# One hybrid decoder layer on eight cores: from two passes of 1024 tokens to one pass of 2064 with weights read once

## The chip, the cores and the metric

The kernel runs on the eight NeuronCores of one Trainium2 chip. Every core does the whole layer for one prompt of 2048 tokens and for 16 decode ("sample") tokens; the cores do not talk to each other. The metric is the device time of the slowest core in microseconds (us), so a few microseconds lost on one core in eight are lost for all.

A program on all eight cores has a second, slower state in some of its executions. Ratios are the mean time of one kernel's fast runs over that of the other's fast runs of the same rounds, so they are not quite the ratio of the medians quoted beside them.

Engines are named as in the profile: PE does matmuls, PEld loads their weights, DVE, ACT and POOL do the elementwise work, SP issues DMA.

## The reference

```python
D_MODEL = 1024; BATCH = 8; SEQ = 2048; DEC_BATCH = 128; D_FF = 2816; EPS = 1e-6
POOL_WINDOWS = (2, 4, 8, 16)

def layer(x, pool_prev, w_in, g_mix, w_pool, s_pool, w_s, b_s, g_v,
          w_pool_out, w_gmlp_out, w_out, g_ffn, w_gate, w_up, w_down):
    h = rmsnorm(x, g_mix)
    proj = h @ w_in                              # 3584 columns: a 512, u 512, v 512, gates 2 x 1024
    a, z = proj[..., :o1], jax.nn.gelu(proj[..., o1:o2])
    gate_a, gate_b = jax.nn.sigmoid(proj[..., o2:o3]), jax.nn.sigmoid(proj[..., o3:])
    pa = pool_mixer(seq_a, pos0, w_pool, s_pool)   # causal means over 2, 4, 8, 16 rows, minus the row,
                                                   # then a 128 x 128 matrix per group, times s_pool
    sg, v = spatial_gating(z, w_s, b_s, g_v)       # u * (causal 128 x 128 mix of rmsnorm(v) + b_s)
    x = x + (gate_a * (pa @ w_pool_out) + gate_b * (sg @ w_gmlp_out)) @ w_out
    h2 = rmsnorm(x, g_ffn)
    x = x + (jax.nn.silu(h2 @ w_gate) * (h2 @ w_up)) @ w_down
    return x, new_pool, v
# then y = rmsnorm(x, g_final); the last 15 rows of a and the normalised v rows are outputs too
```

I call the part up to `pa` and `sg` stage A, then come the gate stage, w_out, and the FFN (gate and up, then down).

## The kernel before

It works in two passes of 1024 tokens (the first takes the 16 samples along) and reads every weight twice. Weights come through a ring of four 8 KB slots, in blocks cut out of the original fp32 arrays and cast to bf16 by the DMA; a slot is refilled when the block in it has been used. The order of every engine is the order in which the program text emits the instructions.

```python
TPS = 1024; NSUP = SEQ // TPS; NSLOT = 4
blocks = []
for s in range(NSUP):
    for cb in (2, 0, 1):
        blocks.append([(0, 8, 512, win_v[:, :, cb * 512:(cb + 1) * 512])])
    ...                                                        # cut: gates, w_pool_out, w_out
    for j in range(NF // 2):
        blocks.append([(0, 8, 256, wgate_v[:, :, j * 256:(j + 1) * 256]),
                       (2048, 8, 256, wup_v[:, :, j * 256:(j + 1) * 256])])
    ...                                                        # cut: w_down
for s in range(NSUP):
    tts = [(i, 128, i * 128) for i in range(8)]                # token tiles of 128
    nts = [(0, 512, [0, 1, 2, 3]), (512, 512, [4, 5, 6, 7])]   # token blocks of 512 columns
    if s == 0:
        tts.append((8, NSMP, TPS)); nts.append((TPS, NSMP, [8]))   # the 16 samples
    ...
    for j in range(NF // 2):                                   # FFN, two rows of 128 at a time
        for fl in range(2):
            for ni, (c0, W, tl) in enumerate(nts):
                bG, bU = h_mm(gw, uw, hres, fl, c0, W, tl)     # 8 + 8 matmuls of W columns
                h_evac(f, c0, W, bG, bU)                       # silu on ACT, product on DVE
        ring_release(hj)
```

The norm takes ACT (sum of squares), DVE (mean plus eps), POOL (`pow`, -0.5), DVE (scale), PE (8 transposes) and ACT (copy out).

## Time and profile before

| | |
|---|---|
| time, median of 3 runs | 885.39 us (880.47 to 886.75) |
| profiled execution, slowest core | 882.3 us |
| PE busy | 94% |
| HBM read | 129.8 MB per core |

The first fence is from the page of the slowest core: busy time per engine, then the span in 40 equal slices of 22 us (each digit is the busy share in tenths; PEclk is the granted PE clock in tenths), the bytes, and the chain of work that ended last.

```profile
PE 830.3 (94%) x4584; PEld 392.5 (44%) x4584; DVE 366.0 (41%) x601; ACT 247.1 (28%) x448; POOL 142.6 (16%) x174
PE   1689999999999999999997999999999999999996
PEclk9989999999999999999999999999999999999999
DMA  8995336666884746266367951567678475455304
HBM read 129.76 MB, written 9.01 MB: 157 GB/s over the span
PE 88%; DMA 5%; DVE 3%; issue 1%; SPq 1%; ACT 1%; POOL 1%; DVEq 0%; POOLq 0%; ACTq 0%
```

PE is nearly always busy, the chain is 88% PE, and DMA is half idle outside the first slices. So the span is PE work plus the places where PE is kept from it. The next fence is the timeline of PE: start, duration, what, and in brackets the idle time before it with what ended it. The rows are from the start, from the boundary of the two passes, and the last one.

```profile
36.33 16.98 PE L346 MATMUL ps<-ring,hT 128*128 128x512 bf16 x72
57.59 6.28 PE L346 MATMUL ps<-hT,ring 128*128 128x512 bf16 x24 [3.94 <-DMA ring<-w_in]
...
77.33 1.89 PE L346 MATMUL ps<-hT,ring 128*128 128x512 bf16 x8
79.06 0.39 PE L638 MATMUL ps<-wsT,ovl 128*128 128x128 bf16 x4
...
480.71 0.61 PE L396 MATMUL ps<-ident_b,hb 128*128 128x128 bf16 x8 [1.45 <-DVE ms L360]
484.04 1.01 PE L396 MATMUL ps<-ident_b,hb 128*128 128x128 bf16 x8 [2.73 <-DVE ms L360]
...
865.76 7.93 PE L346 MATMUL ps<-ring,ovl 128*128 128x512 bf16 x36
```

The first projections start at 36 us and stop again, and PE is dense only from 57.6 us. Eight matmuls of 512 columns take 79.06 - 77.33 = 1.73 us, so the pitch (the time from the start of one to the start of the next) is 216 ns; the mean duration of one (379 ns in the groups by form) is latency, as they overlap. PE ends at 873.7 and the span at 882.3, which is a tail of 8.6 us. At the boundary of the passes there are gaps of 1.45 and 2.73 us, and the clock drops after them. The view of stretches shows that (columns: stretch, its length, busy time and count of PE, PEld, DVE, ACT, POOL, then granted clock, DMA share, GB/s):

```profile
480.60:487.00 6.40, 3.56 (x22) 2.07 (x23) 3.51 (x6) 5.46 (x9) 5.13 (x6) 0.65 0.95 311
```

### The profile page before, as it was taken

The page shows a single profiled execution, that of the slowest core. Times are in us where ns is not written, and L with a number is a line of the kernel's source. Part 1 is how long each engine was busy: PE and PEld are TensorE (multiplying, and loading weights), DVE is VectorE, ACT ScalarE, POOL GpSimd, SP SyncE. Part 2 cuts the span into 40 slices and gives each one's busy share as a digit, 9 for nine tenths or more (in the row PEclk, how much of TensorE's full clock was granted, in tenths as well). Part 3 has the DMA queues.
Part 4 walks back from the last instruction along what each step waited for, and adds up shares of the span by engine and source line. Part 5 has one row for each costly group of instructions (what it writes and reads, how often), then busy time and mean ns, then how long its engine had stood idle before and what let it go on. Part 6 is the DMA issues. An engine that isn't in the chain of part 4 may idle for free.

```text
span 882.3 us, 13022 instructions; the slowest of 8 cores (876.1 to 882.3 us)
## 1 busy us (share of the span) xinstructions
PE 830.3 (94%) x4584; PEld 392.5 (44%) x4584; DVE 366.0 (41%) x601; ACT 247.1 (28%) x448; POOL 142.6 (16%) x174
## 2 busy tenths in 40 slices
PE   1689999999999999999997999999999999999996
PEld 1334444445444444444443444444544444444442
DVE  2448544447322211134557594434631212114446
ACT  3643422225311111120126543222441111110012
POOL 2420011021201010000225201201120101000003
PEclk9989999999999999999999999999999999999999
DMA  8995336666884746266367951567678475455304
GB/s 209 201 141 66 72 39 74 79 102 91 95 97 51 94 51 82 40 93 96 48 139 243 155 66 25 73 82 103 80 87 104 54 90 72 60 84 84 60 18 174
DMA packets 102482, 81.05 MB, mean 92 GB/s; under 512 B 5324, under 2 KB 96964, under 8 KB 102403
## 3 DMA queue, kind: packets, MB, share of 16 engines
q0 software_dynamic: 94048, 58.10, 51.6%
q1 hardware_dynamic: 7390, 20.88, 7.4%
q10 hardware_dynamic: 981, 1.24, 0.6%
q8 instruction: 38, 0.62, 0.3%
q14 instruction: 25, 0.20, 0.1%
HBM read 129.76 MB, written 9.01 MB: 157 GB/s over the span
## 4 chain that ended last, share of the span: by engine, by line
PE 88%; DMA 5%; DVE 3%; issue 1%; SPq 1%; ACT 1%; POOL 1%; DVEq 0%; POOLq 0%; ACTq 0%
PE ps L346 86%; DMA ring<-w_in 2%; DMA xbuf<-xs 2%; PE ps L396 1%; SPq L304 1%; DVE hb L384 1%; DVE ps L644 1%; ACT hT L404 0%; POOL rs L364 0%; DVE shr L536 0%; DVE shr L544 0%; DVE ovl L549 0%; DVE ovl L649 0%; PE ps L593 0%; DVEq L917 0%
## 5 line engine op out<-in xcount | busy, mean ns | idle before, releaser
L346 PE MATMUL ps<-hT,ring 128*128 128x512 bf16 (+1 forms) x2720 | 497.0, 338 | 7.4 <-DMA ring<-w_in 3.9
L346 PEld LDWEIGHTS ps<-hT,ring 128*128 128x128 bf16 x2720 | 228.0, 98 | 263.3 <-issue 11.5
L346 PE MATMUL ps<-ring,ovl 128*128 128x512 bf16 (+1 forms) x1020 | 224.3, 379 | 0.0
L739 DVE TENSOR_TENSOR ovl<-ftmp,ps 128x512 bf16<-128x512 f32 (+1 forms) x110 | 62.3, 583 | 248.4 <-PE ps L346 245.1
L346 PEld LDWEIGHTS ps<-ring,ovl 128*128 128x128 bf16 (+1 forms) x1020 | 97.7, 97 | 118.8 <-issue 4.3
L737 ACT ACTIVATE ftmp<-ps 128x512 f32<-128x512 f32 (+1 forms) x110 | 56.6, 514 | 246.2 <-PE ps L346 246.1
L355 ACT ACTIVATE junk<-xbuf 128x1024 bf16<-128x1024 f32 (+1 forms) x47 | 49.6, 1055 | 139.4 <-DVE xbuf L861 60.7
L364 POOL TENSOR_TENSOR rs<-ms,mhalf 128x1 f32<-128x1 f32 (+1 forms) x68 | 55.5, 819 | 176.4 <-DVE ms L360 176.4
L825 DVE TENSOR_TENSOR xbuf<-xbuf,ps 128x512 f32<-128x512 f32 (+1 forms) x68 | 46.7, 687 | 54.7 <-PE ps L346 54.7
L346 PE MATMUL ps<-ovl,ring 128*128 128x512 bf16 (+1 forms) x320 | 63.2, 337 | 0.0
L707 DVE TENSOR_TENSOR shr<-shr,ps 128x512 f32<-128x512 f32 (+1 forms) x40 | 23.4, 584 | 91.9 <-PE ps L346 91.9
L396 PE MATMUL ps<-ident_b,hb 128*128 128x128 bf16 (+1 forms) x272 | 23.8, 239 | 33.7 <-DVE hb L384 29.3
L267 POOL DMA_DIRECT2D ring<-w_gate x22 | 19.5, 884 | 209.7 <-PE ps L346 209.7
L404 ACT ACTIVATE hT<-ps 128x1024 bf16<-128x1024 bf16 (+1 forms) x34 | 32.3, 966 | 51.3 <-PE ps L396 51.2
L693 ACT ACTIVATE shr<-ps 128x512 f32<-128x512 f32 (+1 forms) x40 | 20.6, 514 | 88.5 <-PE ps L346 87.2
L346 PEld LDWEIGHTS ps<-ovl,ring 128*128 128x128 bf16 x320 | 27.2, 97 | 30.2
L267 POOL DMA_DIRECT2D ring<-w_in x22 | 19.5, 896 | 126.8 <-PE ps L346 116.6
L396 PEld LDWEIGHTS ps<-ident_b,hb 128*128 128x128 bf16 (+1 forms) x272 | 19.3, 108 | 42.1 <-issue 38.6
L267 POOL DMA_DIRECT2D ring<-w_down x12 | 10.3, 858 | 146.0 <-PE ps L346 146.0
L346 PE MATMUL ps<-ring,hT 128*128 128x512 bf16 (+1 forms) x136 | 33.3, 409 | 0.0
L861 DVE TENSOR_TENSOR xbuf<-xbuf,ps 128x512 f32<-128x512 f32 (+1 forms) x34 | 23.2, 683 | 21.7 <-PE ps L346 21.7
L700 ACT ACTIVATE shr<-ps 128x512 f32<-128x512 f32 (+1 forms) x40 | 20.6, 514 | 34.0 <-PE ps L346 33.9
(76 smaller groups left out, 378.9 us busy)
## 6 DMA issues: line engine op xcount, KB each, us to landing
ring<-w_gate POOLq DMA_DIRECT2D x22, 512.0 KB, 8.5
ring<-w_up POOLq DMA_DIRECT2D x22, 512.0 KB, 10.8
xbuf<-xp SPq DMA_DIRECT2D x16, 512.0 KB, 8.7
ring<-w_in POOLq DMA_DIRECT2D x16, 512.0 KB, 10.4
ring<-w_down POOLq DMA_DIRECT2D x8, 1024.0 KB, 10.2
ring<-w_in POOLq DMA_DIRECT2D x6, 1024.0 KB, 18.9
yp<-ybuf SPq DMA_DIRECT2D x11, 512.0 KB, 3.2
ring<-w_out POOLq DMA_DIRECT2D x4, 1024.0 KB, 13.4
```

What stands on the lines that cost most here:

```text
L267: (lambda e, dst=dst, src=src: e.dma_start(out=dst, in_=src)),
L346: ins = e.matmul(out=out, lhsT=lhs_fn(i), rhs=rhs_fn(i), start=(i == 0), stop=(i == n - 1))
L355: P.op('act', lambda e: e.activation(out=junk[:R, ji, 0:width], in_=src_ap, func=AF.Square, accum_out=ss[:R, k:k + 1]), reads=list(src_res ...
L364: P.op('pool', lambda e: e.tensor_tensor(out=rs[:R, k:k + 1], in0=ms[:R, k:k + 1], in1=mhalf[:R, 0:1], op=ALU.pow), reads=[('ms', k), 'mha ...
L396: ins = e.transpose(out=PSB[b][:, kc, :R], in_=hb[:R, hi, kc * 128:(kc + 1) * 128], identity=ident_b[:R, :R])
L404: P.op('act', lambda e: e.activation(out=dst, in_=src, func=AF.Copy), writes=[('hT', slot, 0), ('hT', slot, 1), ('ps', b)])
L693: P.op('act', lambda e, bA=bA, gi=gi, W=W: e.activation(out=gab[:, gi, 0, :W], in_=PS[bA][:, :W], func=AF.Sigmoid), reads=[], writes=[('ga ...
L707: P.op('dve', lambda e, bP=bP, gi=gi, W=W: e.tensor_tensor(out=gab[:, gi, 0, :W], in0=gab[:, gi, 0, :W], in1=PS[bP][:, :W], op=ALU.mult), ...
L737: P.op('act', lambda e: e.activation(out=ftmp[:, fi, :W], in_=PS[bG][:, :W], func=AF.Silu), reads=[], writes=[('ftmp', fi), ('ps', bG)])
L739: P.op('dve', lambda e: e.tensor_tensor(out=actT[:, f, c0:c0 + W], in0=ftmp[:, fi, :W], in1=PS[bU][:, :W], op=ALU.mult), reads=[('ftmp', f ...
L825: P.op('dve', lambda e: e.tensor_tensor(out=xbuf[:R, slot, half * 512:(half + 1) * 512], in0=xbuf[:R, slot, half * 512:(half + 1) * 512], ...
L861: P.op('dve', lambda e, b=b, half=half: e.tensor_tensor(out=xbuf[:R, slot, half * 512:(half + 1) * 512], in0=xbuf[:R, slot, half * 512:(ha ...
```

## The change

The intent is one pass over all 2064 tokens. x stays in SBUF in fp32 from start to end, every weight is read once, in units of 128 x 1024 that the host has packed contiguously (512 KB in HBM, 256 KB in SBUF), w_pool is multiplied into w_pool_out on the chip, and the order of the instructions on each engine comes from a list scheduler with modelled durations. The gate and FFN stages take the tokens in blocks of 416 columns instead of 512 and 16. The core of the diff (cuts marked with `...`; about 1,900 lines in full):

```diff
-TPS = 1024
-NSUP = SEQ // TPS
-NSLOT = 4
+TOK = SEQ + NSMP
+FGROUPS = ((0, 6), (6, 8), (14, 8))
+BLK = [(0, 416), (416, 416), (832, 416), (1248, 416), (1664, 400)]
...
+    def schedule(self, bank_free0):          # list scheduler: of all operations whose inputs are
+        ...                                  # ready, each engine takes the one that can start first;
+                k = (t0, o.prio, i)          # among equals the lower prio; durations are modelled
...
-        ring = sb("ring", [128, NSLOT, SLOT_ELEMS], BF16)
+        X = sb("X", [128, NT + 1, XW], F32)
+        ring = sb("ring", [128, 12, 1024], BF16)
...
+        def load_unit(u, slot, prio, after=()):
+            slots[u] = slot
+            return dma('pool', ring[:, slot, :], wpk[UIDX[u], :, :], 'w%d' % slot, 524288, prio, after)
+        def take(u, prio, after=()):          # the oldest free slot; give(u) puts it back
+            s_ = pool_slots['order'].pop(0)
+            return load_unit(u, s_, prio, after)
...
+        xload(0)
+        dma('act', gmix, cst[:, C_GMIX:C_GMIX + 1024], 'c1', 524288, -9)
+        xload(1); xload(2); xload(3)         # then units a0..a3, v0..v3, u0..u3, all after x tile 0
...
+                P.add('dve', lambda e: e.tensor_tensor_scan(out=W, data0=d0, data1=d1, ...))  # window sums
...
+                        mm(pt, lambda p: p[:, :], [(wpTb[:, g, :], U(('po', g))[:, ...])], ...)  # w_pool fold
...
+        for k in range(8):
+            take(('wo', k), 2000.0)
+        pv = sample_fm(...)                   # the 16 samples as moving columns: 8 x 8 matmuls of 16 columns
+        for t in [0, 1, 2, 3, NT] + list(range(4, NT)):
+            ...                               # for tiles 0 to 3: rows 0 to 4 of w_out first, 5 to 7 later
+            norm(t, gffn, pr + 1.0)
+        for k in range(8):
+            give(('wo', k))
+        pool_slots['order'] += [8, 9, 10, 11]
+        for gi, (f0, nf) in enumerate(FGROUPS):
+            for f in range(f0, f0 + nf):
+                take(('wg', f), base + 10.0 * fl)
+                take(('wu', f), base + 10.0 * fl)
+                for bi, (c0, W) in enumerate(BLK):
+                    ...                       # as before: 8 + 8 matmuls, silu, product
+                give(('wg', f)); give(('wu', f))
+            ...                               # w_down of this group, then the next group
...
+            if o_.start < 45000.0:            # where the model sees PE idle in the first 45 us:
+                ...                           # dummy matmuls on zeros
```

The norm loses its DVE step: an extra column of x holds the eps.

## The prediction

> **What bounds it now.** TensorE: the page says PE 94% busy, the chain of waits is 88% PE. In the timeline 128x512 matmuls follow each other every 216 ns (8 in 1.73 us), 16-column ones every 25 ns, transposes every 56 ns. From the groups by form: 3604 x 0.216 + 612 x 0.025 + 272 x 0.056 + about 7 us of small ones = 816 us of PE work in an 882 us span. The other 66 us: the start (at 57.6 us, after a weight wait of 3.9, about 20 us of work is done: 38 lost), 7 more until 100 us, about 8 at the boundary of the passes (475 to 487 us, half clock granted for 6.8 us), 8.5 of tail, 4 elsewhere. Weight traffic is no bound: DMA is half busy outside the start, so halving it saves nothing by itself.
>
> **What the change does.**
> 1. PE work. 2064 tokens go as 4x416+400 columns instead of 4x512+16. The Trainium skill, "TensorE: Matmul & The Clock Gate" (section "Wait — 56ns, not 53.3ns?"), gives N/2.4 + 2.5 ns; the trace's 216 ns at 512 agrees. Estimate: 872 ns per weight tile against 889, over 544 gate and FFN tiles: -9 us. The 60 sample matmuls of 512 columns (13 us) become 240 of 16 columns and transposes (8 us): -5. w_pool folding: -2. New PE work about 800 us.
> 2. Start. x0 to x3 and 12 weight units: with x4 to x7 and constants 9.5 to 11.5 MB are read by the end of the first 512 tokens. From packet times (4 KB x packets 201 ns; cast packets 68 and 114 ns for 512 and 1024 B, so near 200 estimated for 2048 B) about 330 GB/s: 30 to 38 us, overlapping 24 us of PE work. Loss about 20 us instead of 45 (start plus stage A).
> 3. Stage A afterwards: per 512 tokens PE 24 us, DVE about 22 us (norms 1.28, evictions 0.69 to 0.75, scans estimated at 1.25). Nearly balanced: 6 us of stalls.
> 4. The boundary between passes disappears: -8.
> 5. New: the first w_gate/w_up units take the ring slots of w_out 0 and 1, which are read until the last w_out tile. PE waits for a whole load, estimated 5 us; that skill page (an idle gap over about 3 us returns the clock to half) lets me expect 6.8 us at half clock, as this trace shows after gaps: +8.5.
> 6. The tail stays at 8 us.
>
> Sum: 800 + 20 + 6 + 8.5 + 8 + 3 (other) = 845 us.
>
> **Prediction: 845 us, 80% range 829 to 864. Faster by over 2%: 0.92; within 2%: 0.06; slower by over 2%: 0.02.**
>
> **What would show it.** PE dense from about 36 us (activity slices); 416-column matmuls at a pitch of 176 ns; HBM read falling from 130 MB to about 72; no gap in mid-span, but one of about 5 us before the first silu, released by the DMA of a weight unit, with a clock dip after it; DVE 80 to 95% busy in the first 110 us.
>
> **What would make it wrong.** Each engine's order is fixed from modelled times. If DMA or DVE are slower than modelled (scan over 2 us, slow pow), engines wait for each other in stage A and 10 to 25 us go. Weight loads waiting for slots share a queue with the pow and can delay norms. A denser PE could draw a lower granted clock. If the start streams better than estimated, about 830.

## The result

The new kernel takes 851.01 us (median of 4 runs, 850.65 to 851.83), the old one 886.07 us (4 runs, 880.47 to 892.12). Executions in which one die ran at a lower clock are left out of the means. The ratio is 0.9612, with a 95% interval of 0.9567 to 0.9656: 3.9% faster. The prediction was 845 us, with a range of 829 to 864.

The same lines of the page of the slowest core, after:

```profile
PE 817.4 (96%) x4836; PEld 438.4 (52%) x4876; DVE 351.6 (41%) x565; ACT 236.7 (28%) x440; POOL 98.7 (12%) x185
PE   7989999999999989999999999999999999999994
PEclk8999999999999999999999999999999999999998
DMA  8970045121212160043331033131300441310333
HBM read 69.97 MB, written 9.01 MB: 93 GB/s over the span
PE 81%; DMA 7%; issue 5%; DVE 3%; ACT 2%; POOL 1%; SPq 0%; POOLq 0%; ACTq 0%; DVEq 0%
```

HBM read fell from 129.8 to 70.0 MB, DMA is two thirds idle, and PE is dense from the second slice on (dummy matmuls included). The timeline of PE in the same places (core 4, the slowest): start, the first gates, the step to w_out, the step to the FFN, and the end.

```profile
2.01 7.72 PE L946 MATMUL ps<-actr 128*128 128x512 bf16 x28 [2.01 <-DVE mrg L488]
17.56 2.53 PE L437 MATMUL ps<-hT,ring 128*128 128x128 bf16 x32
41.90 1.05 PE L700 MATMUL ps<-wsT,mrg 128*128 128x128 bf16 x16 [0.54 <-DVE mrg L473]
...
132.69 2.98 PE L437 MATMUL ps<-hT,ring 128*128 128x416 bf16 x16
135.50 1.57 PE L437 MATMUL ps<-actr,ring 128*128 128x416 bf16 x8
...
300.42 8.58 PE L437 MATMUL ps<-ring,mrg 128*128 128x512 bf16 x39
312.09 3.79 PE L437 MATMUL ps<-ring,mrg 128*128 128x512 bf16 x9 [3.08 <-DMA ring<-wpk]
...
369.98 1.57 PE L437 MATMUL ps<-hT,ring 128*128 128x416 bf16 x8
371.73 0.61 PE L595 MATMUL ps<-ident_b,hb 128*128 128x128 bf16 x8 [0.18 <-DVE hb L473]
375.67 0.61 PE L595 MATMUL ps<-ident_b,hb 128*128 128x128 bf16 x8 [0.52 <-DVE hb L473]
...
827.76 8.80 PE L437 MATMUL ps<-ring,actr 128*128 128x512 bf16 x39
```

The first row is the dummy matmuls, the first real projection starts at 17.56 us, and at 41.90, when the spatial matmuls start, the projections of the first 512 tokens are done. 16 matmuls of 416 columns take 135.50 - 132.69 = 2.81 us, a pitch of 176 ns. The gap of any size in mid-span is the 3.08 us at 312 us, on a weight DMA of w_out. Before the first FFN rows there are 0.18 and 0.52 us only. The stretches around that one gap, and before them the stages of the whole span (columns as before):

```profile
17.50:132.70 115.20, 106.84 (x742) 58.31 (x754) 81.39 (x153) 75.23 (x152) 27.33 (x47) 0.99 0.50 115
132.70:300.40 167.70, 167.67 (x963) 94.02 (x962) 70.57 (x120) 42.91 (x82) 10.71 (x21) 1.00 0.23 34
300.40:370.00 69.60, 65.95 (x441) 33.49 (x448) 40.39 (x51) 31.19 (x48) 11.05 (x21) 0.98 0.19 34
370.00:836.50 466.50, 464.80 (x2647) 246.78 (x2663) 151.82 (x227) 80.04 (x149) 41.89 (x80) 1.00 0.27 53
...
309.00:312.10 3.10, 0.01 (x2) 0.04 (x2) 0.00 (x0) 0.00 (x0) 0.00 (x0) 1.00 1.06 172
312.10:315.60 3.50, 3.50 (x9) 1.28 (x10) 1.37 (x2) 0.09 (x1) 0.00 (x0) 0.53 0.61 112
```

DMA is saturated in the gap, and the clock is near half after it. The gap splits the cores: on cores 1, 3, 4 and 7 it is 3.1 to 3.5 us and their spans are 847.7 to 848.8, on the other four it is 0.6 to 1.5 us and the spans are 843.7 to 844.9.

Pitches times counts, against the measured stretches of the two profiled executions, give the account. PE work in a stretch is my sum from the pitches (216, 176, 56 and 25 ns for 512, 416, 128 and 16 columns); the loss is the stretch minus that.

| loss in us | before | predicted | after |
|---|---|---|---|
| PE work, all stages | 816 | 800 | 800 |
| start and stage A | 45 | 26 | 30 (until 132.7; work 103) |
| boundary of the passes | 8 | 0 | 0 |
| gate stage | | 0 | 0 (167.7; work 167.5) |
| step to w_out, w_out | | 0 | 4.6 (69.6; work 65) |
| step to the FFN, FFN | | 8.5 | 2 (466.5; work 464.5) |
| tail after the last matmul | 8.6 | 8 | 12.3 |
| other | 4 | 3 | |
| span | 882 | 845 | 849 |

The stretches in the last column are 132.7, 167.7, 69.6, 466.5 and 12.3, which sum to the span of 848.8. So of 33.5 us in the spans, about 16 are PE work that is gone and the rest is idle time that is gone, and the weight bytes have no row of their own. The sum was right to 4 us, but several of its terms were not. The experiments test the PE work, the start, the two steps and the tail. No run undoes the single pass, so the 8 us of the boundary and the 15 us of the start are read from the two traces alone.

### The profile page after: what moved, and what is told of

Its sections match the earlier page's. It is cut to its first block, busy times and chain, and to the rows that moved or that the text cites. A ratio compares the mean times of both kernels' runs of the same rounds, so it can differ in the third digit from the quotient of the medians.

```text
span 848.8 us, 13201 instructions; the slowest of 8 cores (843.7 to 848.8 us)
## 1 busy us (share of the span) xinstructions
PE 817.4 (96%) x4836; PEld 438.4 (52%) x4876; DVE 351.6 (41%) x565; ACT 236.7 (28%) x440; POOL 98.7 (12%) x185
## 4 chain that ended last, share of the span: by engine, by line
PE 81%; DMA 7%; issue 5%; DVE 3%; ACT 2%; POOL 1%; SPq 0%; POOLq 0%; ACTq 0%; DVEq 0%
PE ps L437 79%; DMA ring<-wpk 4%; DMA X<-xs 2%; POOL rs L575 1%; DMA mrg<-cst 1%; ACT junk L458 1%; DVE X L468 1%; DVE hb L473 1%; PE ps L595 1%; PE ps L824 1%; SPq L492 0%; ACT hT L458 0%; PE ps L946 0%; POOL ring L492 0%; DVE actr L473 0%
## 5 line engine op out<-in xcount | busy, mean ns | idle before, releaser
L437 PE MATMUL ps<-hT,ring 128*128 128x416 bf16 (+5 forms) x2777 | 486.7, 334 | 1.7 <-ACT hT L458 1.3
L458 ACT ACTIVATE Fb<-ps 128x416 f32<-128x416 f32 (+4 forms) x228 | 117.7, 519 | 473.0 <-PE ps L437 375.6
L468 DVE TENSOR_TENSOR actr<-Fb,ps 128x416 bf16<-128x416 f32 (+2 forms) x126 | 75.2, 598 | 241.0 <-PE ps L437 233.1
L437 PE MATMUL ps<-ring,actr 128*128 128x512 bf16 x686 | 151.2, 379 | 1.0
L468 DVE TENSOR_TENSOR X<-X,ps 128x512 f32<-128x512 f32 (+1 forms) x132 | 88.6, 684 | 76.5 <-PE ps L437 76.5
L492 POOL DMA_DIRECT2D ring<-wpk x110 | 58.7, 540 | 521.4 <-PE ps L437 510.2
L437 PEld LDWEIGHTS ps<-ring,actr 128*128 128x128 bf16 x704 | 68.6, 98 | 81.9
L458 ACT ACTIVATE junk<-X 128x1025 bf16<-128x1025 f32 (+1 forms) x51 | 54.1, 1062 | 88.0 <-DVE X L468 76.6
L437 PE MATMUL ps<-ring,mrg 128*128 128x512 bf16 x256 | 61.3, 387 | 4.7 <-DMA ring<-wpk 4.3
L437 PE MATMUL ps<-actr,ring 128*128 128x416 bf16 (+1 forms) x320 | 62.4, 338 | 0.0
L473 DVE SCALAR_TENSOR_TENSOR hb<-X,rs,actr 128x1024 bf16<-128x1024 f32 (+1 forms) x17 | 21.8, 1282 | 18.5 <-POOL rs L575 17.7
```

The source lines that it names most:

```text
L437: ins = e.matmul(out=ap, lhsT=l, rhs=rr, start=(start and i == 0), stop=(stop and i == len(pairs) - 1))
L458: return e.activation(out=P.r(out), in_=P.r(in_), func=func, scale=scale, **kw)
L468: return P.add(eng, lambda e: e.tensor_tensor(out=P.r(out), in0=P.r(a), in1=P.r(b), op=op), reads=[a, b], writes=[out], dur=vdur(n, 1.04), ...
L473: return P.add('dve', lambda e: e.scalar_tensor_tensor(out=P.r(out), in0=P.r(a), scalar=sc, in1=P.r(b), op0=op0, op1=op1), reads=rd, write ...
L492: return P.add(q, lambda e: e.dma_start(out=out, in_=in_), reads=[in_], writes=[out], dur=(900.0 if q == 'pool' else 1000.0), lat=0.0, pri ...
```

## The experiments

All gave correct results. Each is an edit of the new kernel (whose scheduler then makes a new order) and ran beside the kernel before on the same chip. Differences below are of medians, against 851.0 for the new kernel in the first two batches of runs and 851.4 in the last batch, in which the new kernel itself was repeated. In the first two it was not, and they ran on two chips on which the kernel before took 884.1 and 886.0 us (886.1 beside the new kernel), so differences under about 2 us in these two batches say no more than "about the same":

> The new kernel once more, unchanged, on the same chip and in the same rounds as the two runs that follow, for the comparison with them: 851 us within 1 us.

Measured: 851.39 us (5 runs, 850.93 to 851.76).

### Blocks of 512 and 16 columns

```diff
-BLK = [(0, 416), (416, 416), (832, 416), (1248, 416), (1664, 400)]
+BLK = [(0, 512), (512, 512), (1024, 512), (1536, 512), (2048, 16)]
```

> The new kernel with token blocks of 4x512+16 columns instead of 4x416+400 in the gate and FFN stages, all else the same. Theory (a matmul costs columns/2.4 ns plus a fixed part, so 544 weight tiles cost 889 instead of 872 ns each): +9 us against the new kernel, so about 860 us, spread evenly over the gate and FFN stages. Rival (the width of the blocks does not matter, the gain came from the start and the vanished boundary): within 1 us of 851.

Measured: 859.20 us (858.97 to 860.32), +8.2; its ratio to the kernel before is 0.9714 [0.9693, 0.9735]. The width of the blocks is worth what the pitches say, and where they say it: averaged over the cores of the two profiles, the gate stage takes 2.8 us longer and the FFN 5.3. Both ways use five matmuls per weight tile and the same 2064 columns. The difference is the remainder: the pitches of 216 ns at 512 columns and 176 at 416 would give about 9 ns for 16 columns (my estimate from these two), and the trace of the kernel before shows 25; 16 ns times 544 is 8.7 us.

### The samples as a 17th tile again

```diff
-        pv = sample_fm(...); act(samW, pv, AF.Copy, 2000.6, n=128)
...
-                sample_back(samW, pr)
+                for h in range(2):
+                    pt = pt_()
+                    mm(pt, lambda p: p[:NSMP, :], [(merged[:, k, SEQ:TOK], U(('wo', k))[:, h * 512:(h + 1) * 512])
+                                                   for k in range(8)], pr)
+                    ...                     # and the same with w_down, in each of the three groups
```

> The new kernel with the 16 sample tokens in w_out and w_down again as a 17th tile: 60 matmuls of 512 columns in place of 240 of 16 columns with transposes back. Theory (60 x 0.216 = 12.9 us of PE against 240 x 0.0255 and 16 fp32 transposes at 0.112, 7.9 us): +5 us, about 856. Rival (loading the weights of 240 small matmuls eats the gain, or the transposes back sit on the critical path): within 2 us.

Measured: 857.13 us (856.25 to 858.40), +6.1, a little more than the 5 of the theory; the ratio is 0.9672 [0.9611, 0.9732]. With the run before, 14 us of the gain were taken back by two edits that change mainly what PE executes (the other engines' share of the same blocks and samples changes with it).

### FFN weights read twice

```diff
+            if u[0] in ('wg', 'wu', 'wd'):
+                dma('sp', dump[:, :], wpk[UIDX[u], :, :], 'q4', 524288, prio, [o_])   # dump: dead part of SBUF
```

> The new kernel, but each of the 66 FFN weight units is read from HBM a second time, into dead space, right after its own load. Theory (halving the weight traffic is worth nothing by itself, as no engine waits for weights in the FFN): HBM read rises from 70 to about 104.6 MB and the time stays at 851 within 1 us. Rival (weight traffic costs time, by contention between the cores): 34.6 MB of the 60 MB that the change saved come back, so at least +5 us.

Measured: 851.39 us (850.90 to 852.39), +0.4, with this line on its page:

```profile
HBM read 104.57 MB, written 9.01 MB: 134 GB/s over the span
```

34.6 of the 59.8 MB that the change saved are read again, and the time does not move. Less traffic in the FFN is not where the gain came from; the other 25 MB, those of the start among them, were not tested in this way.

### FFN rows 4 and 5 not hoisted

```diff
+                dep = [last_wo] if f in (4, 5) else []
-                take(('wg', f), base + 10.0 * fl)
+                take(('wg', f), base + 10.0 * fl, dep)     # and wu
```

> The new kernel, but the loads of FFN rows 4 and 5, which the list scheduler had hoisted ahead of rows 0 to 3 because their ring slots are free early, wait for the last w_out matmul. Theory (the stall predicted at the first silu exists, and only the hoisting hides it): a PE wait of 4 to 6 us on a weight DMA before the first silu and a clock dip after it; the wait between the gate stage and w_out (3.1 us) shrinks, since four units fewer compete there; in all +3 to +8 us on 851. Rival (FFN weights are there in time for another reason): no wait over 1 us before the first silu, time within 2 us of 851.

Measured: 855.35 us (854.74 to 855.93), +4.3; the ratio is 0.9669 [0.9645, 0.9693]. The timeline of PE (slowest core) at the two steps:

```profile
308.57 2.54 PE L437 MATMUL ps<-ring,mrg 128*128 128x512 bf16 x11 [1.22 <-DMA ring<-wpk]
...
368.19 0.61 PE L595 MATMUL ps<-ident_b,hb 128*128 128x128 bf16 x8 [1.59 <-DVE hb L473]
373.20 1.01 PE L595 MATMUL ps<-ident_b,hb 128*128 128x128 bf16 x8 [4.40 <-DVE hb L473]
```

The view of stretches for the time after the second step (columns as before):

```profile
374.30:380.00 5.70, 5.65 (x19) 2.58 (x20) 0.00 (x0) 3.01 (x4) 2.12 (x5) 0.57 1.03 140
```

The predicted stall is there: 6.0 us, and then 5.7 us at a clock of 0.57. The profile names the last tiles' norm as its releaser, not the weight DMA: the transposes stand in front of the FFN matmuls in PE's order, and both arrive late because PE has nothing to put in between. The weights would have held PE as long by themselves: in the trace the first w_gate unit lands at 374.21, 7.1 us after its issue, and the first FFN matmul starts at 374.35. From the last w_out matmul to the last matmul of all, the mean over the cores is 473.5 us here and 466.3 in the new kernel, 7.2 more. In return the wait at the step to w_out fell from 3.08 to 1.22 us. So the scheduler had moved FFN rows 4 and 5, whose ring slots come free after the gate stage, ahead of rows 0 to 3, which I had taken to come first; that filled the hole I predicted, and their loads opened the smaller one at w_out.

### w_out units first

```diff
+                dep = [wo_used] if f in (4, 5) else []      # wo_used: the last w_out matmul of tile 3
-        dma('sp', gffn, cst[:, C_GF:C_GF + 1024], 'c5', 524288, 1900)
         for k in range(8):
-            take(('wo', k), 2000.0)
+            wo_last = take(('wo', k), 2000.0)
+        dma('sp', gffn, cst[:, C_GF:C_GF + 1024], 'c5', 524288, 1900, after=[wo_last])
```

> The new kernel, but between the gate stage and w_out the last w_out units have the DMA queues to themselves: the hoisted loads of FFN rows 4 and 5 wait until the first four w_out tiles are done, and the g_ffn load waits for the last w_out unit. Theory (the 3.1 us wait of PE there, which brings a clock dip of 3.4 us on some cores, is bandwidth taken by those five loads): the wait falls to about 1 us, no dip, and as the slowest cores are those with the dip, -2 to -4 us, so 847 to 849. Rival (the wait is the latency of a load that can only start when the gate stage ends): wait stays near 3 us and the time within 1 us of 851. The FFN rows still come in time, so no wait before the first silu.

Measured: two runs, 848.79 and 847.67 us, -2.8 against 851.0. Two runs are few; the run with both repairs, below, tests the same edit again. The step to w_out on its slowest core:

```profile
308.37 4.69 PE L437 MATMUL ps<-ring,mrg 128*128 128x512 bf16 x21 [1.30 <-DMA ring<-wpk]
```

The wait fell to 1.30 us and the clock dip there is gone on all cores. The three loads of w_out that are left took a median of 5.8 us from issue to landing, where the seven loads of the new kernel took 10.7. The gap was bandwidth taken by loads that were not urgent. The run before, which held back only the four FFN units, had a wait of 1.22 us here, so these four are enough to explain it.

### Without the dummy matmuls

```diff
-                n_ = int((gap - 200.0) / 235.0) if gap > 700.0 else 0
+                n_ = 0
```

> The new kernel without its 46 dummy matmuls on zeros in the first 50 us. Theory (they keep the granted clock up): without them the first 20 us of real matmuls run partly at half clock, +1 to +4 us. Rival (they stand in front of real work: the first projection starts 2.5 us after its input is ready): -1 to -3 us. If both hold they cancel, within 1 us.

Measured: 851.82 us (851.44 to 854.19), +0.8, which is not told from zero. The two effects cancel. The first projection starts at 16.22 us on its slowest core instead of 17.56, and its first 32 matmuls then take 3.4 us instead of 2.4. The traces' first record of full clock stands at 17.7 to 21.6 us on the eight cores here, and at 4.8 to 7.9 us in the new kernel.

### Another start

```diff
-        dma('act', gmix, cst[:, C_GMIX:C_GMIX + 1024], 'c1', 524288, -9)
-        xload(1)                              # and 2, 3
+        dma('sp', gmix, cst[:, C_GMIX:C_GMIX + 1024], 'c1', 524288, -9.95)
+        xload(1, after=[x_dma[0]])            # and 2, 3
+        act(tmp16[:, 0:1], mhalf[:, :], AF.Square, -20.0)     # loads the ACT table early
-                n_ = int((gap - 200.0) / 235.0) if gap > 700.0 else 0
+                n_ = int((gap - 200.0) / 235.0) if gap > 700.0 and (t_ < 8000.0 or t_ > 30000.0) else 0
```

> The new kernel with another start: a tiny activation loads the ACT table before the first x tile is there (it took 1.28 us after it), g_mix goes right after x tile 0 on the same queue, x tiles 1 to 3 only after tile 0 has landed, and the dummy matmuls that stand between the first real transposes are gone. Theory (the first 17.5 us are a chain x0, table load, norm, g_mix, transposes, not bandwidth): the first projection matmul starts near 12 us instead of 17.6, and 3 to 5 us of it reach the end, so about 847. Rival (the first 50 us are bound by the bytes of the first weights): it starts earlier but waits for weights after it, within 1 us of 851.

Measured: 852.44 us (851.59 to 853.29), +1.4. The theory fails, and the wait that the rival names is there. Three rows of PE from core 4: the first projection, then a wait for a weight unit near the end of the first 512 tokens, then the spatial matmuls that follow it.

```profile
13.97 1.01 PE L437 MATMUL ps<-hT,ring 128*128 128x128 bf16 x8 [3.78 <-DMA ring<-wpk]
...
39.60 1.89 PE L437 MATMUL ps<-hT,ring 128*128 128x512 bf16 x8 [1.67 <-DMA ring<-wpk]
41.32 1.06 PE L701 MATMUL ps<-wsT,mrg 128*128 128x128 bf16 x16
```

The chain of latencies did get shorter (10.2 us to the first transposed tile), but PE then waited 3.78 us for the first weight unit and 1.67 us for the last. The spatial matmuls of the first 512 tokens start at 41.90 us in the new kernel, at 41.32 here (44.18 on the slowest core) and at 42.21 without dummies. On core 4 the last of its twelve weight units lands at 39.23 us in the new kernel and at 39.36 here, though it was issued 2.6 us earlier. Whatever the start, the first block ends when its bytes are there. How fast they come depends on more than their number, as the last experiment shows.

### The last roots off POOL, three runs

A "root" is the `pow` with -0.5 in a norm. A "drain" is the instruction that the trace calls DRAIN, which closes an engine's work.

The span of the new kernel ends long after its last store. The closing instructions in the traces show why; these rows are from the traces themselves, as the views leave such instructions out (times in us from the span's start, on the slowest core of each profile):

```
kernel                     last matmul ends   POOL drain starts, takes   last store waited for   span ends
before                          873.7            876.17   1.81                881.8                882.3
after                           836.6            838.82   9.73                843.6                848.7
roots of 17 tiles off POOL      837.1            751.96   9.69                848.0                848.6
roots of 2 tiles off POOL       837.8            833.60   9.73                848.3                848.9
```

In the new kernel POOL's work closes with a drain that starts with the last `pow` (838.82 and 838.85 us) and takes 9.73 us on all eight cores (1.81 in the kernel before), so it ends 5 us after the last store has landed. First edit: all 17 roots of the last stage on ACT and DVE.

```diff
+            if eng == 'dve':
+                act(rs[:R, k:k + 1], ss[:R, k:k + 1], AF.Sqrt, prio)
+                P.add('dve', lambda e: e.reciprocal(rs[:R, k:k + 1], rs[:R, k:k + 1]), ...)
+                return rs[:R, k:k + 1]
             P.add('pool', lambda e: e.tensor_tensor(..., op=ALU.pow), ...)
```

> The new kernel with the last 17 reciprocal roots on ACT (square root) and DVE (reciprocal) instead of the pow on POOL. Theory: in the new kernel the span ends with POOL's closing drain, which took 9.73 us on every core (1.81 us in the kernel before) and starts only when POOL's last pow is issued; with no POOL work after the last weight load it starts some 70 us earlier and is hidden, so the tail after the last matmul falls from 12.3 to 7.5 to 8.5 us and the time by 4 to 5 us, to about 846.5. Rival (the drain waits for the end of the other engines or for the last stores): tail and time unchanged within 1 us.

Measured: 850.54 us (849.17 to 851.10), -0.5, where the theory forecast -4 to -5. The drain moved to 752 us and was hidden, as the theory said, so it does not wait for the other engines or the last stores, as the rival had it. But the tail is still 11.5 us: DVE's fixed order puts the reciprocal and the scaling of one tile in front of the adds of the next, so each tile waits for the square root of the one before, and the last add started at 841.2 us, 4 us after PE was done.

Second edit: only the last two tiles' roots leave POOL, so that the work before them is as it was.

```diff
-                    r = rstd(X[:R, t, 0:D + 1], R, 1.0 / 32.0, pr)
+                    r = rstd(X[:R, t, 0:D + 1], R, 1.0 / 32.0, pr, 'dve' if t in (14, 15) else 'pool')
```

> The new kernel with only the reciprocal roots of the last two tiles moved from POOL to ACT and DVE. In the run that moved all 17 the drain was hidden, but ACT's and DVE's fixed order then let the adds of one tile wait for the root of the tile before, and the tail stayed at 11.4 us. Theory (both effects are what the trace showed): here POOL's last pow is that of tile 13, the drain ends before the last store lands, and the chain after the last matmul stays at about 7.5 us: -4 to -5 us, about 846.5. Rival (moving the roots costs as much as the drain): within 1 us of 851.

Measured: 850.32 us (849.76 to 850.99), -1.1 against 851.39. The forecast of -4 to -5 is missed, and the rival is right: moving the roots costs nearly as much as the drain did. The drain is hidden, but the tail is still 11 us instead of 12. The timeline of ACT and DVE on the slowest core, after PE's end at 837.8:

```profile
837.55 1.28 ACT L458 ACT_TABLE_LOAD   x1
838.84 0.20 ACT L458 ACTIVATE rs<-ss 128x1 f32<-128x1 f32 x1
839.15 0.16 DVE L577 RECIPROCAL rs<-rs 128x1 f32<-128x1 f32 x1 [2.31 <-ACT rs L458]
840.68 0.68 DVE L468 TENSOR_TENSOR X<-X,ps 128x512 f32<-128x512 f32 x1
```

The square root needs another ACT table, 1.28 us, in the middle of the tail, and the last add again waits for the tile before. `pow` on DVE might have avoided both, but did not compile.

Both repairs together, the edit of "w_out units first" and this second edit:

> Both repairs together: the w_out units first, and the last two roots off POOL. Theory (the two lie in different stages and add up): -3.5 and -4.6, about 843. Rival (they overlap, or the tail is set by the slowest core alone): no better than the better of the two, 846 to 848.

Measured: 846.60 us (845.87 to 847.19), -4.8 against 851.39 in the same rounds; the ratio to the kernel before is 0.9556 [0.9530, 0.9582]. This is the fastest version. It misses the 843 of the theory and lies in the range that the rival named, but for another reason than the rival's: the edits don't get in each other's way. In the same rounds the second edit alone gave -1.1, so "w_out units first" is worth 3.7 beside it, clear of the ranges of both and more than the 2.8 of its two runs. Only the second gain is smaller than expected.

### What the drain depends on

```diff
-            return dma('pool', ring[:, slot, :], wpk[UIDX[u], :, :], 'w%d' % slot, 524288, prio, after)
+            dma('pool', ring[:, slot, 0:512], wpk[UIDX[u], :, 0:512], 'w%d' % slot, 262144, prio, after)
+            return dma('pool', ring[:, slot, 512:1024], wpk[UIDX[u], :, 512:1024], 'wb%d' % slot, 262144, prio, after)
```

> The new kernel with every weight unit loaded by two DMA instructions of 512 columns, on two semaphores, instead of one of 1024: a look at what POOL's closing drain of 9.73 us depends on. If it grows with the number of POOL DMA instructions or of their semaphores: 15 to 20 us. If it depends on the pieces being large (the kernel before had pieces of 512 and 1024 B and 1.81 us): below 5 us. If on neither: 9.7 us. The time is not the point.

Measured: a drain of 9.32 us on all cores (one look, 859.5 us). Twice the DMA instructions and semaphores did not lengthen it, and pieces of half the size hardly shortened it. What makes it 9.7 us here and 1.8 in the kernel before stays open.

The time says something too, though it is one execution: with the same bytes, the kernel is 8 us slower. The loss is mostly at the start. The spatial matmuls of the first 512 tokens begin at 44.5 to 50.0 us on the eight cores, against 40.3 to 42.1 in the new kernel, and PE's waits for weight units on the slowest core are 11.5 us in all, against 4.3. A packet of the casting loads takes 98 ns (median) for 1024 B and 173 ns for 2048 B, so half the size is more than half the time, and POOL issues twice as many loads at about 0.55 us each. So at the start the size of the pieces counts, and not the bytes alone. The kernel before loaded its weights in pieces of 512 and 1024 B, so the packing of the weights may have a share in the gain at the start; no run tells how large.

## Why the prediction was right

The total was right because the largest steps were, those about PE work, the start and the boundary. That it came within 4 us of the span is partly luck: terms that were 9.5 us too high and terms that were 13 us too low nearly cancelled.

- **"Weight traffic is no bound ... halving it saves nothing by itself."** Right for the FFN: reading 34.6 MB again cost 0.4 us, which is not told from zero. It was not tested for the rest.
- **"New PE work about 800 us."** Right. The sum over the stretches is 800. The block width gave 8.2 us back when it was undone (predicted 9), the samples 6.1 (predicted 5). The w_pool part (predicted 2) was not tested by itself. The rule N/2.4 + 2.5 ns of the Trainium skill ("TensorE: Matmul & The Clock Gate", section "Wait — 56ns, not 53.3ns?") holds in this trace at 416 columns (176 ns measured).
- **"Loss about 20 us instead of 45" and "6 us of stalls".** The mechanism was right and the size 4 us too small: 30 instead of 26. The bytes bound the first block, as estimated: reading was to take 30 to 38 us, and the last weight unit of the first block released PE at 39.6 us in the run that waited for it. The stalls after it are where the 4 us are: predicted at 6, they are 6.8 us of gaps in PE from 41.9 to 132.7 us on core 4 and 2.6 us of dummy matmuls (12 of 216 ns) that fill further waits, 9.4 in all, which leaves about 20 for the start, as predicted. The profile puts 2.9 us of the gaps down to DVE, 2.4 to ACT and 1.2 to a weight load. And DVE was not as full as I had said: it was busy 81.4 of the 115.2 us from 17.5 to 132.7, which is 71% and not 80 to 95%. So these are waits for single results, of DVE and of ACT, and not the work of one full engine. The scan took 1.23 to 1.26 us (estimated 1.25).
- **"The boundary between passes disappears: -8."** Right by the traces: no gap or dip of that kind is left. No run tested it by itself.
- **"New: the first w_gate/w_up units take the ring slots of w_out 0 and 1 ... PE waits for a whole load ... +8.5."** This step failed. I read the order of execution from the order of the loops, in a kernel whose order a scheduler makes. Units 0 and 1 do wait, but rows 4 and 5 sit in slots that are free earlier, and were run first. The run with those two rows held back has the stall, with 6.0 us and a dip, 7.2 us in all of the 8.5 predicted. So its size was right; that nothing would fill it was not, and the last tiles' norm holds PE there as long as the load does. What the hoisting cost was a smaller hole that I did not see ("no gap in mid-span"): 3.08 us and a dip at the step to w_out on the slowest core, with gaps of 3.1 to 3.5 us on the four slowest.
- **"The tail stays at 8 us."** This step failed too: 12.3. The chain of work after the last matmul is as short as before (7 us to the landing of the last store), but POOL's drain now outlasts it. The trace of the kernel before showed that drain, at 1.81 us; nothing in it told that it would grow.
- **"PE dense from about 36 us"**: real matmuls are dense from 17.6 us, but with dummies among them and narrow blocks, so the step was not wrong in its effect: the first block ended at 41.9.

Terms that came out lower (the FFN step, -6.5, and the 3 for "other", which the stretches contain) and higher (start and stage A about +4, w_out +4.6, tail +4.3) left 849 in place of 845 for the profiled span. The 851 of the runs is that span plus what lies outside it, about 2 us.

## What to carry to other kernels

When PE is 94% busy, count its columns and its idle stretches, and give bytes a price only where the trace shows PE waiting for them: here 34.6 MB more in the FFN cost nothing that could be measured, while half-size loads cost 6 us in the first block (one execution), and 8 us came from a block width that leaves no remainder of 16 columns. In a kernel whose order a scheduler makes, ask which work it can pull into a hole before you charge for the hole, and then ask what the pulled loads take from the loads that are urgent at that moment. Look at the last instructions of every engine, not only at the chain of work: an engine's closing drain can end the span, and it starts only when that engine's last instruction is issued.

## What the Trainium skill lacked or had wrong

- "TensorE: Matmul & The Clock Gate", Part 1, tells one to budget 13/16 of the clock for dense matmuls on all cores. These runs were at full clock in the fast state: the stretches of the gate stage and the FFN show a granted clock of 1.00, and the means over the span were 0.984 to 0.996. Only single stretches of 3.7 to 5.1 us at 0.81, which is that 13/16, appeared, between 30 and 41 us, on some cores of three runs. Which power profile the chips had is not on record.
- The same page, section "Back-to-back issue gap", gives a sustained 131 ns for a matmul of 512 columns and 81 ns for 128. Here the pitch is 216 ns and, for transposes, 56 ns, which fits the page's other rule, N/2.4 + 2.5 ns.
- The same page says ("Why this matters for your kernels") that an idle gap of over about 3 us brings half clock. It held roughly: between the first 60 us and the last matmul the dips lasted 3.4 or 6.8 us, and at the step to w_out a gap of 3.08 us was enough on core 4, while core 0 with 0.58 us had none. But the length of the gap alone did not decide: core 1 of the same execution had 3.08 us and no dip, and when the new kernel was repeated, 2.36 us on core 3 and 2.33 on core 6 brought one. In the kernel before, two gaps of 1.45 and 2.73 us with only transposes between were enough too.
- "ScalarE: Activation LUTs", section "What ACT_TABLE_LOAD costs", gives 1283 ns for the load and about 2.66 us for a switch, with a drain counted in. In the trace the load takes 1.28 us and the square root starts at its end (837.55 to 838.84), so 1.28 us is what the tail paid after it began.
- No page tells of a closing drain of POOL that takes microseconds: 1.81 us before, 9.73 after, 9.32 with half loads, the same on all cores of each of these runs, about the same when it starts right after the last load (9.69 to 10.02), and the last thing to end in the span when POOL's last `pow` comes with the last tile.
